# Sliding windows stored from the middle of a row: a 28-element shift between two channel halves

## The chip, the cores and the metric

The kernel runs on one core of a Trainium2 chip, alone. Its time is the device time of one execution in microseconds; a number for a kernel is the median over runs. All tensors are float32. Nothing is computed beyond copying, so TensorE has no work.

## The reference

An image batch is cut into overlapping windows of 8 x 8 pixels, 4 apart, and every window is written out with all of its channels:

```python
x: (16, 64, 64, 64)                     # batch, channels, height, width
n_h = n_w = (64 - 8) // 4 + 1           # 15
result = zeros((16, 15, 15, 64, 8, 8))
for i in range(15):
    for j in range(15):
        result[:, i, j] = x[:, :, 4*i:4*i+8, 4*j:4*j+8]
```

The input has 16.78 MB, the output 58.98 MB: 3600 windows (b, i, j) of 64 channels x 64 pixels, that is 16 KB each and contiguous in the output. Windows of one image follow each other by i and then j.

## The kernel before

**Where the input lies.** One tile `L` holds all of the input: 128 partitions = 2 channel halves (`ch`, 64 partitions each) x 16 images x 4 quarters of the height (`hq`); a partition has 32 channels x 16 rows x 64 columns, 128 KB. So a window row index i is 4*hq + s with a slot s of 0 to 3: for s = 0, 1, 2 the 8 pixel rows lie inside a quarter, for s = 3 the lower 4 of them lie in the next partition (next quarter), and quarter 3 has no such window.

**Loads.** The first 4 channels of each half (`FC`) come in by 8 DMAs of 64 partitions, ScalarE's queue for half 0 and SyncE's for half 1, into two of the four output buffers used as staging (`S`), partitions 32 to 95. The other 28 channels come in by loads of 8 partitions each straight into `L`, from SyncE's queue and from POOL's (`load`, L58); every row is 4 KB. The images are taken as two sets of 8 (`y`). The staging copies (L126) then move the 4 channels from `S` to `L`, half 0 on ScalarE and half 1 on VectorE, each in two instructions, one for each `y`.

**Stores.** Four buffers `G` of 128 partitions x 16 KB are filled in turn; each partition of a buffer is one whole window, 64 channels. A buffer is stored by one indirect DMA from POOL (`scatter`, L138), which sends each partition's 16 KB to the output row that an index tile names; rows out of bounds are dropped. There are up to eight DMAs of POOL in flight, each with its own semaphore.

**Filling.** Early tiles (`part`) need only one set of 8 images: 32-partition copies, 3 on ScalarE and 5 on VectorE (L196). Three of them come first for y = 0, three later for y = 1, alternating with plain tiles. In a tile of `unit`, a plain one (s = 0) holds slot 0 in its lower 64 partitions and slot 1 in the upper ones; a crossing one (s = 2) holds slots 2 and 3 at one column j. A half of the partitions has only half of the channels, so each 64-partition half of a tile is filled from both channel halves by `fill`: one copy stays in its partitions, the other goes across 64 partitions. ScalarE's copies are L158; VectorE's across are shuffles (L168), with a quarter of the channels going to ScalarE (L172). For slot 3 the lower 4 rows come by a shuffle that moves data one partition up (L161). The last column's slots 0 and 1 are stored by two plain SyncE DMAs of 64 partitions (32 to 95).

**Order.** Nothing but the program order, the buffers' turn and the scheduler of the framework sets the order: each engine works down its list, and a copy into a buffer waits until the store four tiles earlier has landed.

Of the kernel before, what the change touches and what calls it, by code (L numbers as in the profile page):

```python
# [10 lines left out]
def kernel(  # L11
# [19 lines left out]
    CH = 2  # L31
    HQ = P // (B * CH)
    CL = C // CH
    RB = H // HQ
    NSLOT = RB // ST
    NWIN = NH * NW
    CFREE = C * WS * WS
    HP = P // CH
    YB = 8
    NY = B // YB  # L40
    QP = YB * HQ
    assert HQ == 4 and WS == 2 * ST and QP == 32 and NSLOT == 4
# [22 lines left out]
    pi, tb, tq, tc_, th, idx, idx_y0, idx_y1, idx_lo, idx_hi = (  # L65
        itile(n) for n in ("pi", "tb", "tq", "tc", "th", "idx", "idx_y0", "idx_y1", "idx_lo", "idx_hi")
    )
    FAR = float(2 * B * NWIN)
# [8 lines left out]
    def tt(d, a, b, op):  # L77
        nc.vector.tensor_tensor(out=d[:, :], in0=a[:, :], in1=b[:, :], op=op)  # L78

    bits(tb, 2, B - 1)  # L80
    bits(tq, 0, HQ - 1)
    bits(tc_, 6, 1)
    mul(tb, tb, NWIN)
    mul(th, tq, NSLOT * NW)
    tt(tb, tb, th, ALU.add)
    mul(th, tc_, NW)
    tt(idx, tb, th, ALU.add)

    bits(th, 5, 1)
    mul(idx_y0, th, 1 - YB * NWIN)  # L90
    tt(idx_y0, idx_y0, idx, ALU.add)
    nc.vector.tensor_scalar(out=idx_y1[:, :], in0=idx_y0[:, :], scalar1=float(YB * NWIN), scalar2=None, op0=ALU.add)

    nc.vector.tensor_scalar(out=tq[:, :], in0=tq[:, :], scalar1=float(HQ - 1), scalar2=FAR, op0=ALU.is_equal, op1=ALU.mult)
    tt(th, tc_, tq, ALU.mult)
    tt(idx_hi, idx, th, ALU.add)
    nc.vector.tensor_scalar(out=tc_[:, :], in0=tc_[:, :], scalar1=-1.0, scalar2=1.0, op0=ALU.mult, op1=ALU.add)
    tt(th, tc_, tq, ALU.mult)
    tt(idx_lo, tb, th, ALU.add)
    mul(th, tc_, NW)  # L100
    tt(idx_lo, idx_lo, th, ALU.add)


    NG = 4
    G = [gpool.tile([P, C, WS, WS], f32, name=f"G{n}") for n in range(NG)]
    FC = C * WS * WS // (RB * W)
    S = [g.rearrange("p c r w -> p (c r w)").rearrange("p (c r w) -> p c r w", c=FC, r=RB) for g in G[NG - CH :]]
# [14 lines left out]
    for y in range(NY):  # L122
        for ch in range(CH):
            f = slice(QP + y * QP, QP + (y + 1) * QP)
            d = slice(ch * HP + y * QP, ch * HP + (y + 1) * QP)
            (nc.scalar.copy, nc.vector.tensor_copy)[ch](out=L[d, 0:FC, :, :], in_=S[ch][f])  # L126

    o_v = out.rearrange("b i j c r w -> (b i j) (c r w)")
    nxt = [min(p + 1, 31) for p in range(32)]

    o_q = out.rearrange("b i j c r w -> i j b (c r w)")
# [5 lines left out]
    def scatter(g, ix, j, s):  # L137
        st = nc.gpsimd.indirect_dma_start(  # L138
            out=o_v,
            out_offset=bass.IndirectOffsetOnAxis(ap=ix[:, 0:1], axis=0),  # L140
            in_=g.rearrange("p c r w -> p (c r w)"),
            in_offset=None,
            element_offset=(s * NW + j) * CFREE,
            bounds_check=B * NWIN - 1,
            oob_is_err=False,
        )
        free(st)

    def fill(g, half, s, j, lo, n, copies):

        d = slice(half * HP + lo, half * HP + lo + n)
        cols = slice(j * ST, j * ST + WS)
        for ch in (half, 1 - half):
            f = slice(ch * HP + lo, ch * HP + lo + n)
            cs = slice(ch * CL, (ch + 1) * CL)
            copy = copies[ch != half]
            if s < NSLOT - 1:
                copy(out=g[d, cs, :, :], in_=L[f, :, s * ST : s * ST + WS, cols])  # L158
            else:
                copy(out=g[d, cs, 0:ST, :], in_=L[f, :, s * ST : RB, cols])  # L160
                nc.vector.stream_shuffle(out=g[d, cs, ST:WS, :], in_=L[f, :, 0:ST, cols], mask=nxt)  # L161

    act, dve = nc.scalar.copy, nc.vector.tensor_copy
    same = list(range(32))


    def shf(out, in_):
        nc.vector.stream_shuffle(out=out, in_=in_, mask=same)  # L168

    def split(k, other):  # L170
        def both(out, in_):
            act(out=out[:, 0:k], in_=in_[:, 0:k])  # L172
            other(out=out[:, k:], in_=in_[:, k:])  # L173

        return both

    mix = split(CL // 4, shf)


    EARLY = 3  # L180
    ACT_C = 12
    at = 0

    def tile_():
        nonlocal at
        at += 1
        return G[(at - 1) % NG]

    def part(y, j):
        g = tile_()  # L190
        for d in range(P // QP):
            s, dj = d // NY, d % NY
            cols = slice((j + dj) * ST, (j + dj) * ST + WS)
            for ch in range(CH):
                f = (ch * NY + y) * QP
                (act if (2 * d + ch) % 3 == 0 else dve)(  # L196
                    out=g[d * QP : (d + 1) * QP, ch * CL : (ch + 1) * CL, :, :],
                    in_=L[f : f + QP, :, s * ST : s * ST + WS, cols],
                )
        scatter(g, (idx_y0, idx_y1)[y], j, 0)  # L200

    crossed = 0

    def unit(j, s, copies=(shf, mix)):
        nonlocal crossed
        g = tile_()
        if s == 0:
            fill(g, 0, 0, j, 0, HP, (act, copies[0]))
            fill(g, 1, 1, j, 0, HP, (act, copies[1]))
            scatter(g, idx, j, s)  # L210
        else:

            turn = 1 - crossed % 2
            crossed += 1
            fill(g, turn, s, j, 0, HP, (act, act))
            fill(g, 1 - turn, s + 1, j, 0, HP, (shf, mix))
            scatter(g, (idx_hi, idx_lo)[turn], j, s)

    for n in range(EARLY):
        part(0, 2 * n)  # L220
    plain = [(j, 0) for j in range(2 * EARLY, NW - 1)]
    cross = [(j, 2) for j in range(NW)]
    for n in range(EARLY):
        part(1, 2 * n)
        unit(*plain.pop(0), (dve, dve))
    while plain:
        for w in cross[:3]:
            unit(*w)
        cross = cross[3:]
        unit(*plain.pop(0), *([] if len(plain) else [(split(ACT_C, shf), split(ACT_C, dve))]))  # L230


    o_e = out.rearrange("b i j c r w -> j b i (c r w)")
    j = NW - 1
    for s in range(2):
        g = tile_()
        cols = slice(j * ST, j * ST + WS)
        for y in range(NY):
            d = slice(QP + y * QP, QP + (y + 1) * QP)
            for ch in range(CH):  # L240
                f = slice(ch * HP + y * QP, ch * HP + (y + 1) * QP)
                for c0, c1, copy in ((0, ACT_C, act), (ACT_C, CL, dve)):
                    copy(out=g[d, ch * CL + c0 : ch * CL + c1, :, :], in_=L[f, c0:c1, s * ST : s * ST + WS, cols])  # L243
        g_q = g.rearrange("p c r w -> p (c r w)")
        free(nc.sync.dma_start(out=o_e[j, :, s : s + (HQ - 1) * NSLOT + 1 : NSLOT], in_=g_q[QP : QP + HP]))


# [33 lines left out]
```

## Time and profile before

| | |
|---|---|
| median of 3 runs | 187.99 us (187.95 to 188.54) |
| profiled execution | 187.89 us |
| its span, first to last instruction | 186.1 us |
| VectorE, ScalarE, POOL busy | 146.8 us (79%), 146.5 us (79%), 47.7 us (26%) |
| DMA packets | 11300, 75.81 MB, mean 407 GB/s |
| POOL's queue, SyncE's, ScalarE's | 86.6%, 10.6%, 1.8% of 16 DMA engines' span |
| landing of a store after its issue on POOL | 9.3 to 15.0 us, median 11.7 |

An execution's time is its span and some 1.8 us around it. Busy shares are of the span; the share of a queue is the time that its packets took, of 16 engines. Line numbers (L158) are those of the kernel's file.

### The profile page before, as it was taken

To read this page: it belongs to the slowest core of one execution; us is meant where nothing else is said; L and a number is where in the kernel's file an instruction comes from. 1 tells how busy PE (TensorE), PEld (TensorE's weight loads), DVE (VectorE), ACT (ScalarE), POOL (GpSimd) and SP (SyncE) were. 2 spreads that over 40 slices of the span, in tenths; PEclk is the share of its full clock that TensorE was granted. 3 is DMA by queue.
4 is the path that set the end of the run, shared out by engine and by line. 5 is a ranking of instruction groups with operands and counts; after the bars stand their busy time and mean duration, and the time that the engine had idled before them with its cause. 6 is when DMAs were issued, how large, how long until landed. Compare 5 with 4: busy or idle time off the path is not lost.

```text
span 186.1 us, 575 instructions
## 1 busy us (share of the span) xinstructions
DVE 146.8 (79%) x205; ACT 146.5 (79%) x96; POOL 47.7 (26%) x50
## 2 busy tenths in 40 slices
DVE  5045008999998969799999999999999999998600
ACT  0069108997999989988899999998998899999600
POOL 7405222006335341422222222222222222223000
DMA  5999999999999999999999999999999999999994
GB/s 165 359 402 403 399 401 400 381 385 424 433 440 423 431 433 430 433 430 433 424 435 419 433 426 423 433 412 433 398 444 396 444 419 409 440 409 433 409 447 204
DMA packets 11300, 75.81 MB, mean 407 GB/s; under 512 B 3600, under 2 KB 3600, under 8 KB 7696
## 3 DMA queue, kind: packets, MB, share of 16 engines
q0 software_dynamic: 9296, 66.86, 86.6%
q1 hardware_dynamic: 1680, 7.86, 10.6%
q10 hardware_dynamic: 320, 1.05, 1.8%
q14 instruction: 4, 0.03, 0.0%
HBM read 16.78 MB, written 62.91 MB: 428 GB/s over the span
## 4 chain that ended last, share of the span: by engine, by line
DMA 41%; DVE 37%; issue 8%; ACT 5%; POOL 2%; ACTq 1%; POOLq 0%; DVEq 0%; PEldq 0%
DVE G L168 16%; DMA out_dram<-G,idx 14%; DMA out_dram<-G,idx_y 13%; DMA L<-in_x_dram 13%; DVE G L161 11%; DVE G L196 10%; ACT G L243 3%; POOL L L58 2%; ACT G L158 1%; ACT G L172 1%; ACTq L276 0%; DVE G L158 0%; POOLq L138 0%; POOL pi L69 0%; POOL out_dram L138 0%
## 5 line engine op out<-in xcount | busy, mean ns | idle before, releaser
L158 ACT COPY G<-L 64x2048 f32<-64x2048 f32 x46 | 87.2, 1896 | 5.8 <-DMA out_dram<-G,idx 3.7
L168 DVE STREAM_SHUFFLE G<-L 64x1024 f32<-64x1024 f32 (+4 forms) x39 | 53.0, 1358 | 1.2
L196 DVE COPY G<-L 32x2048 f32<-32x2048 f32 x30 | 36.6, 1220 | 14.9 <-DMA L<-in_x_dram 12.1
L196 ACT COPY G<-L 32x2048 f32<-32x2048 f32 x18 | 33.9, 1896 | 11.5 <-DMA L<-in_x_dram 10.4
L161 DVE STREAM_SHUFFLE G<-L 64x1024 f32<-64x1024 f32 x30 | 38.4, 1280 | 0.0
L138 POOL DMA_INDIRECT out_dram<-G,idx_y x6 | 10.7, 1776 | 26.7 <-DVE G L196 16.3
L58 POOL DMA_DIRECT2D L<-in_x_dram x16 | 11.9, 760 | 19.5 <-DMA L<-in_x_dram 19.0
L138 POOL DMA_INDIRECT out_dram<-G,idx_lo x8 | 7.7, 963 | 30.9 <-DVE G L161 12.0
L138 POOL DMA_INDIRECT out_dram<-G,idx x8 | 10.4, 1295 | 18.1 <-ACT G L158 9.3
L138 POOL DMA_INDIRECT out_dram<-G,idx_hi x7 | 6.7, 962 | 26.6 <-DVE G L161 19.0
L126 DVE COPY L<-G 32x4096 f32<-32x4096 f32 x2 | 4.6, 2284 | 8.2 <-DMA G<-in_x_dram 8.2
L172 ACT COPY G<-L 64x256 f32<-64x256 f32 (+2 forms) x21 | 10.2, 484 | 0.5
L126 ACT ACT_TABLE_LOAD x1 | 1.3, 1283 | 10.8 <-DMA G<-in_x_dram 10.8
L158 DVE COPY G<-L 64x2048 f32<-64x2048 f32 x6 | 7.3, 1222 | 0.2
L243 DVE COPY G<-L 32x1280 f32<-32x1280 f32 x8 | 6.5, 818 | 0.9 <-DMA out_dram<-G,idx_hi 0.8
L126 ACT COPY L<-G 32x4096 f32<-32x4096 f32 x2 | 7.2, 3604 | 0.0
L243 ACT COPY G<-L 32x768 f32<-32x768 f32 x8 | 6.6, 829 | 0.1
L168 DVE LOAD_MASK_SELECT G<-L x39 | 0.3, 8 | 1.4 <-DMA out_dram<-G,idx_y 1.0
L72 DVE TENSOR_SCALAR tb<-pi 128x1 int32<-128x1 int32 x1 | 0.2, 153 | 1.0 <-POOL pi L69 1.0
L173 DVE COPY G<-L 64x1280 f32<-64x1280 f32 x1 | 0.9, 874 | 0.0
L78 DVE TENSOR_TENSOR th<-tc,tq 128x1 int32<-128x1 int32 x2 | 0.3, 156 | 0.0
L75 DVE TENSOR_SCALAR th<-tc 128x1 int32<-128x1 int32 x2 | 0.3, 154 | 0.0
(21 smaller groups left out, 3.0 us busy)
## 6 DMA issues: line engine op xcount, KB each, us to landing
L<-in_x_dram POOLq DMA_DIRECT2D x10, 896.0 KB, 19.3
L<-in_x_dram SPq DMA_DIRECT2D x6, 768.0 KB
out_dram<-G SPq DMA_DIRECT2D x2, 1024.0 KB, 10.2
G<-in_x_dram ACTq DMA_DIRECT2D x4, 256.0 KB, 8.0
G<-in_x_dram SPq DMA_DIRECT2D x4, 256.0 KB, 8.7
L<-in_x_dram POOLq DMA_DIRECT2D x6, 128.0 KB, 18.2
out_dram<-G,idx POOLq DMA_INDIRECT x8, 13.2
out_dram<-G,idx_lo POOLq DMA_INDIRECT x8, 10.6
```

Of the source, the lines that this page charges most:

```text
L58: eng.dma_start(out=L[p0 : p0 + QP - HQ + 1 : HQ, c0:c1, :, :], in_=x_v[ch, y, q, :, c0:c1, :])
L75: nc.vector.tensor_scalar(out=d[:, :], in0=a[:, :], scalar1=float(m), scalar2=None, op0=ALU.mult)
L78: nc.vector.tensor_tensor(out=d[:, :], in0=a[:, :], in1=b[:, :], op=op)
L126: (nc.scalar.copy, nc.vector.tensor_copy)[ch](out=L[d, 0:FC, :, :], in_=S[ch][f])
L138: st = nc.gpsimd.indirect_dma_start(out=o_v, out_offset=bass.IndirectOffsetOnAxis(ap=ix[:, 0:1], axis=0), in_=g.rearrange("p c r w -> p (c ...
L158: copy(out=g[d, cs, :, :], in_=L[f, :, s * ST : s * ST + WS, cols])
L161: nc.vector.stream_shuffle(out=g[d, cs, ST:WS, :], in_=L[f, :, 0:ST, cols], mask=nxt)
L168: nc.vector.stream_shuffle(out=out, in_=in_, mask=same)
L172: act(out=out[:, 0:k], in_=in_[:, 0:k])
L173: other(out=out[:, k:], in_=in_[:, k:])
L196: (act if (2 * d + ch) % 3 == 0 else dve)(out=g[d * QP : (d + 1) * QP, ch * CL : (ch + 1) * CL, :, :], in_=L[f : f + QP, :, s * ST : s * S ...
L243: copy(out=g[d, ch * CL + c0 : ch * CL + c1, :, :], in_=L[f, c0:c1, s * ST : s * ST + WS, cols])
```

## The change

The two channel halves now lie 28 elements (7 window steps) apart within a partition's row: half 0 starts at element 28 of the tile `Lt`, half 1 at element 0. `LB` views all 128 partitions from element 0. Read through `LB` at column j + 7, the lower partitions give half 0 at column j and the upper ones half 1 at column j + 7: one copy over 128 partitions fills the first half of every partition's 16 KB. The lower partitions' second half is half 1 at column j; the upper partitions' second half is half 0 at column j + 8.

So a lower partition holds the whole window j, and an upper one the second channel half of window j + 7 and the first channel half of window j + 8, which follow each other in the output. The upper partitions therefore store 16 KB from the middle of an output row to the middle of the next. The index tiles count half rows (8 KB). The lower partitions take columns 0 to 6, the upper ones everything from the middle of column 7 to the middle of column 14; what is left over, the first half of column 7 and the second half of column 14, is stored by `singles` in rows of 8 KB. A tile has one slot s; slots 0, 1 and 2 go out in one scatter of 128 partitions, slot 3 in two of 64 partitions (`scatter_x`), since the rows of quarter 3 have to be dropped. Seven tiles are of slot 3. The store from SyncE's queue at the end is now slot 1 at column 6 and its partner.

```diff
-    L = lpool.tile([P, CL, RB, W], f32)
+    JL = NW // 2
+    SH = JL * ST
+    LF = CL * RB * W
+    Lt = lpool.tile([P, LF + SH], f32)
+    L = [Lt[ch * HP : (ch + 1) * HP, SH - ch * SH : SH - ch * SH + LF].rearrange("p (c r w) -> p c r w", c=CL, r=RB) for ch in range(CH)]
+    LB = Lt[:, 0:LF].rearrange("p (c r w) -> p c r w", c=CL, r=RB)
...
     def load(eng, ch, y, q, c0, c1):
-        p0 = ch * HP + y * QP + q
-        eng.dma_start(out=L[p0 : p0 + QP - HQ + 1 : HQ, c0:c1, :, :], in_=x_v[ch, y, q, :, c0:c1, :])
+        p0 = y * QP + q
+        eng.dma_start(out=L[ch][p0 : p0 + QP - HQ + 1 : HQ, c0:c1, :, :], in_=x_v[ch, y, q, :, c0:c1, :])
...
-            d = slice(ch * HP + y * QP, ch * HP + (y + 1) * QP)
-            (nc.scalar.copy, nc.vector.tensor_copy)[ch](out=L[d, 0:FC, :, :], in_=S[ch][f])
+            d = slice(y * QP, (y + 1) * QP)
+            (nc.scalar.copy, nc.vector.tensor_copy)[ch](out=L[ch][d, 0:FC, :, :], in_=S[ch][f])
...
+    def scatter_x(g, s, j):
+        for u in range(CH):
+            hp = slice(u * HP, (u + 1) * HP)
+            st = nc.gpsimd.indirect_dma_start(
+                out=out.rearrange("b i j c r w -> (b i j) (c r w)"),
+                out_offset=bass.IndirectOffsetOnAxis(ap=idx_r[0:HP, 0:1], axis=0),
+                in_=g[hp, :, :].rearrange("p h f -> p (h f)"),
+                in_offset=None,
+                element_offset=(s * NW + j + u * JL) * CFREE + u * HFREE,
+                bounds_check=B * NWIN - 1,
+                oob_is_err=False,
+            )
+            free(st)
...
+    def move(out, src, s, col, copy):
+        cols = slice(col * ST, col * ST + WS)
+        if s < NSLOT - 1:
+            copy(out=out, in_=src[:, :, s * ST : s * ST + WS, cols])
+        else:
+            copy(out=out[:, :, 0:ST, :], in_=src[:, :, s * ST : RB, cols])
+            nc.vector.stream_shuffle(out=out[:, :, ST:WS, :], in_=src[:, :, 0:ST, cols], mask=nxt)
...
+    def cell(s, j, copy=shf):
+        g = tile_()
+        move(win(g, 0, P, 0), LB, s, j + JL, act)
+        move(win(g, 0, HP, 1), L[1], s, j, act)
+        move(win(g, HP, HP, 1), L[0], s, j + JL + 1, act if s == NSLOT - 1 else copy)
+        if s < NSLOT - 1:
+            scatter(g, idx, s, j)
+        else:
+            scatter_x(g, s, j)
...
+    plain = [(s, j) for s in range(2) for j in range(EARLY, JL)] + [(2, j) for j in range(JL)]
+    plain.remove((1, JL - 1))
+    cross = [(NSLOT - 1, j) for j in range(JL)]
...
+    nc_, nt = len(cross), len(plain) + len(cross)
+    for n in range(nt):
+        cell(*(cross if (n + 1) * nc_ // nt > n * nc_ // nt else plain).pop(0))
...
+    singles(0)
+    singles(2)
+    last(1, JL - 1)
```

In the changed file the staging copies are L125, the early copies L196, plain copies and shuffles L172 and L167, crossing copies and shuffles L174 and L175, the scatters L137 and L150.

More of the change, by code (lines that the diff above doesn't have):

```diff
@@ L75, in mul @@
         nc.vector.tensor_scalar(out=d[:, :], in0=a[:, :], scalar1=float(m), scalar2=None, op0=ALU.mult)
[L77 to L100, printed above, removed]
@@ L104 @@
+    rows(idx, tb, 2, B - 1, CH * NWIN)
+    rows(idx, idx, 6, 1, NW)
+    bits(ta, 0, HQ - 1)
+    nc.vector.tensor_scalar(out=ta[:, :], in0=ta[:, :], scalar1=float(HQ - 1), scalar2=FAR, op0=ALU.is_equal, op1=ALU.mult)
+    add(idx_x, idx, ta)
+    rows(idx_r, tb, 2, B - 1, CH * NWIN)
+    mul(idx_r, idx_r, 1 / CH)
+    bits(ta, 0, HQ - 1)
+    nc.vector.tensor_scalar(out=ta[:, :], in0=ta[:, :], scalar1=float(HQ - 1), scalar2=FAR, op0=ALU.is_equal, op1=ALU.mult)
+    add(idx_r, idx_r, ta)
     NG = 4
-    G = [gpool.tile([P, C, WS, WS], f32, name=f"G{n}") for n in range(NG)]
@@ L106 @@
-    FC = C * WS * WS // (RB * W)
-    S = [g.rearrange("p c r w -> p (c r w)").rearrange("p (c r w) -> p c r w", c=FC, r=RB) for g in G[NG - CH :]]
+    G = [gpool.tile([P, CH, HFREE], f32, name=f"G{n}") for n in range(NG)]
+    FC = CFREE // (RB * W)
+    S = [g.rearrange("p h f -> p (h f)").rearrange("p (c r w) -> p c r w", c=FC, r=RB) for g in G[NG - CH :]]
     x_b = x.rearrange("b (ch cl) (hq r) w -> ch hq b cl (r w)", ch=CH, hq=HQ)
@@ L143, in scatter @@
             element_offset=(s * NW + j) * CFREE,
-            bounds_check=B * NWIN - 1,
-            oob_is_err=False,
+            **({} if n > 1 else dict(bounds_check=CH * B * NWIN - 1, oob_is_err=False)),
         )
         free(st)
[L149 to L161, printed above, removed]
+    def scatter_x(g, s, j):
[11 more added lines that the diff above has]
+            free(st)
@@ L163, with win @@
+    def win(g, p0, n, h):
+        return g[p0 : p0 + n, h, :].rearrange("p (c r w) -> p c r w", c=CL, r=WS)
     act, dve = nc.scalar.copy, nc.vector.tensor_copy
-    same = list(range(32))
     def shf(out, in_):
         nc.vector.stream_shuffle(out=out, in_=in_, mask=same)
[L170 to L180, printed above, removed]
@@ L191, in part @@
         for d in range(P // QP):
[L192 to L198, printed above, removed]
-                )
-        scatter(g, (idx_y0, idx_y1)[y], j, 0)
-    crossed = 0
@@ L204, in unit @@
[L204 to L245, printed above, removed]
+            s, u = d // CH, d % CH
@@ new lines, in part @@
+            for h in range(CH):
+                ch = h ^ u
+                col = j + (JL + h if u else 0)
+                src = L[ch][y * QP : (y + 1) * QP, :, s * ST : s * ST + WS, col * ST : col * ST + WS]
+                (act if (2 * d + h) % 3 == 0 else dve)(out=win(g, d * QP, QP, h), in_=src)
+        scatter(g, (idx_y0, idx_y1)[y], 0, j)
+    def cell(s, j, copy=shf):
[7 more added lines that the diff above has]
+            scatter_x(g, s, j)
@@ new lines, with singles @@
+    for n in range(EARLY):
+        part(0, n)
+    plain = [(s, j) for s in range(2) for j in range(EARLY, JL)] + [(2, j) for j in range(JL)]
+    plain.remove((1, JL - 1))
+    cross = [(NSLOT - 1, j) for j in range(JL)]
+    for n in range(EARLY):
+        part(1, n)
+        cell(*plain.pop(0), dve)
+    nc_, nt = len(cross), len(plain) + len(cross)
+    for n in range(nt):
+        cell(*(cross if (n + 1) * nc_ // nt > n * nc_ // nt else plain).pop(0))
+    def singles(s0):
+        g = tile_()
+        for h, s in enumerate((s0, s0 + 1)):
+            move(win(g, 0, P, h), LB, s, CH * JL, act)
+            scatter(g, idx_x if s == NSLOT - 1 else idx, s, JL, 1, h)
@@ new lines, in last @@
+    def last(s, j):
+        o_e = out.rearrange("b i j (h c) r w -> i b (j h c r w)", h=CH)
+        for u in range(CH):
+            g = tile_()
+            for y in range(NY):
+                for h in range(CH):
+                    ch = h ^ u
+                    col = j + (JL + h if u else 0)
+                    src = L[ch][y * QP : (y + 1) * QP, :, s * ST : s * ST + WS, col * ST : col * ST + WS]
+                    for c0, c1, copy in ((0, ACT_C, act), (ACT_C, CL, dve)):
+                        copy(out=win(g, QP + y * QP, QP, h)[:, c0:c1], in_=src[:, c0:c1])
+            at = (CH * j + u * NW) * HFREE
+            free(
+                nc.sync.dma_start(
+                    out=o_e[s : s + (HQ - 1) * NSLOT + 1 : NSLOT, :, at : at + CFREE].rearrange("i b f -> b i f"),
+                    in_=g[QP : QP + HP, :, :].rearrange("p h f -> p (h f)"),
+                )
+            )
```

33 lines of the change are left out of this document (21 added, 12 removed).

## The prediction

> **What bounds the kernel now.** I read the page's slices first, then the busy table by stage, the timeline of the first 60 us, the table of groups by form, and last the DMA queues of the final 2 us. The span is 186.1 us.
>
> The slices of the page; each is 4.65 us wide:
>
> ```profile
> DVE  5045008999998969799999999999999999998600
> ACT  0069108997999989988899999998998899999600
> ...
> DMA  5999999999999999999999999999999999999994
> GB/s 165 359 402 403 399 401 400 381 385 424 433 440 423 431 433 430 433 430 433 424 435 419 433 426 423 433 412 433 398 444 396 444 419 409 440 409 433 409 447 204
> ```
>
> The DMA row is 9 in every slice but the first and the last. VectorE and ScalarE are full too, but only from slice 17 on, and the transfer rate hardly moves when they fill up: the transfers set the time, and the engines only have to keep them fed. The table by stage puts rates to it (last two columns: share of the 16 DMA engines, GB/s):
>
> ```profile
> 24.00:28.00 4.00, 0.00 (x0) 0.00 (x0) 1.27 (x2) 1.00 1.03 400
> 40.00:44.00 4.00, 3.91 (x4) 4.00 (x3) 1.40 (x1) 1.00 1.06 387
> 80.00:90.00 10.00, 9.66 (x18) 8.70 (x8) 1.92 (x2) 1.00 1.01 431
> 100.00:140.00 40.00, 39.36 (x63) 38.55 (x28) 8.66 (x9) 1.00 1.00 422
> 182.40:184.20 1.80, 0.00 (x0) 0.00 (x0) 0.00 (x0) 1.00 0.84 355
> ```
>
> Loads (4 KB rows) run at 400 GB/s, stores (16 KB rows) at 431. Nothing is idle between them: 16.78 MB of loads end near 45.4 us (16.2 MB by 44 us in the 4 us windows, the rest at 390), and the first store is issued before that. So any microsecond in which no transfer is queued, and any loss of rate, goes to the end in full. How tight the handover is shows in the timeline:
>
> ```profile
> 10.83 1.28 ACT L126 ACT_TABLE_LOAD   x1 [10.83 <-DMA G<-in_x_dram]
> 11.82 4.60 DVE L126 COPY L<-G 32x4096 f32<-32x4096 f32 x2 [8.17 <-DMA G<-in_x_dram]
> 12.13 7.23 ACT L126 COPY L<-G 32x4096 f32<-32x4096 f32 x2
> ...
> 28.47 16.98 ACT L196 COPY G<-L 32x2048 f32<-32x2048 f32 x9 [9.11 <-DMA L<-in_x_dram]
> 28.49 24.92 DVE L196 COPY G<-L 32x2048 f32<-32x2048 f32 x20 [12.07 <-DMA L<-in_x_dram]
> ...
> 42.14 1.40 POOL L138 DMA_INDIRECT out_dram<-G,idx_y  x1 [9.72 <-ACT G L196]
> ```
>
> The staging copies (L126) run at 11 to 19 us, while both engines have nothing else. At 28.47 the lower images' first channel half has landed and the window copies begin: 9 on ScalarE at 1.887 each, 20 on VectorE at 1.246 each (gaps included). Store 1 needs seven of ScalarE's nine: 28.47 + 13.2 = 41.7, and it is issued at 42.14, from where about 2.6 us pass until its bytes move.
>
> The prices by form:
>
> ```profile
> L158 ACT COPY G<-L 64x2048 f32<-64x2048 f32 x46 | 87.2, 1896 | 5.8 <-DMA out_dram<-G,idx 3.7 <-DVE G L161 0.6 <-DMA out_dram<-G,idx_hi 0.4
> L161 DVE STREAM_SHUFFLE G<-L 64x1024 f32<-64x1024 f32 x30 | 38.4, 1280 | 0.0
> L196 ACT COPY G<-L 32x2048 f32<-32x2048 f32 x18 | 33.9, 1896 | 11.5 <-DMA L<-in_x_dram 10.4 <-DMA out_dram<-G,idx_y 0.8
> L172 ACT COPY G<-L 64x768 f32<-64x768 f32 x2 | 1.7, 829 | 0.1
> ```
>
> A copy on 32 partitions costs what one on 64 does (1896 ns): the time goes by elements per partition, so I price 128 partitions the same.
>
> **Part 1, the copies: cheaper, and hidden.** A plain tile now takes ScalarE two copies (128 and 64 partitions, 2 x 1.90 = 3.8 us) and VectorE one shuffle (2.43 us), against 4.87 us for its 2.10 MB at 431 GB/s. A crossing tile takes ScalarE 3 x 1.04 (1024 elements, interpolated between 829 and 1896 ns) and VectorE 3 x 1.28 = 3.84 us; before, VectorE had about 4.85 us of shuffles for each crossing tile, whose 112 rows (1.84 MB) move in 4.26 us, so from 80 us on it fell slowly behind. What that relief can be worth is the difference between 431 and 422 GB/s from 100 to 180 us, 80 x 9/431 = 1.7 us at the most, and nothing if the rate falls for another reason. I take 1.0. The bytes are the same, 58.98 MB out. The index arithmetic (25 small instructions for 20, about 0.15 us each) and POOL's seven extra scatters (0.96 us each, engine 26% busy) lie under transfers: nothing.
>
> **Part 2, the staging copies move.** In the instruction order that the changed program is built with, they are no longer first. ScalarE's first one now waits for all loads of its half and images (queues of POOL and SP), not for its staging loads alone, and so does VectorE's; the two halves being flat slices of one tile, the dependency tracking sees an overlap that the bytes don't have. So the table load and the staging copy go onto the path at 28.47: 1.28 + 7.23/2 = 4.9 us. Both engines' window copies queue behind it, since VectorE's first copy waits for that ScalarE copy. From 33.4 us: ScalarE's seventh window copy ends at 33.4 + 7 x 1.887 = 46.6, store 1 is issued at 47.0, its bytes move at 49.6. The loads are over at 45.4: **a first hole of 4.2 us**, where there was none.
>
> A second follows. Stores 1 to 3 (6.29 MB) last 14.6 us, to 64.2. Store 3's buffer is also staging room: two of its VectorE copies wait until ScalarE's second staging copy has read it, which now stands after all nine window copies: 33.4 + 17.0 + 3.6 = 54.0. Then VectorE has these two (56.5), one copy for tile 4, its own second staging copy (2.3), and four more copies: 56.5 + 1.25 + 2.3 + 5.0 = 65.0. Store 4 is issued at 65.1, moves at 67.7: **3.5 us of hole**. From there tiles come every 3.8 to 5.7 us with stores 5 and 6 already queued behind; no further hole. Sum 7.7 us, all on the path.
>
> **Part 3, crossing stores come in two.** Each of seven crossing tiles is stored by two scatters of 64 partitions, 0 to 63 and then 64 to 127, 48 valid rows (0.79 MB) each. Before, every store of this size spanned both halves; no row shows a store from one half only. At the full 431 GB/s one takes 1.82 us and the price is nothing. The other bound: if a half is served by half of the SBUF's paths, 216 GB/s, 3.65 us, 1.82 more, 14 times: 25.5 us. What rows are near? The final SP stores have 64 partitions, but 32 to 95:
>
> ```profile
> q1 hardware_dynamic: 48, 0.66, 81.3%
> ```
>
> From 182.4 to 184.3 this queue alone holds 81% of the 16 engines, so 64 rows are spread over all of them, four each; two half stores would then stand one behind the other on every engine, not side by side on two sets. The nearest one-sided rows are the loads of the upper half: POOL saw three of them land at 19.08, 24.93 and 31.12 us, 0.92 MB every 5.9 to 6.2 us, some 150 GB/s, well below the half rate, with the other half's loads beside them making up the 400. I take that a one-sided store runs at less than full rate, and three quarters of the extra, since an engine that is ahead already reads the second half while another is on the first: 14 x 1.4 = 19.6 us.
>
> [...]
>
> **Smaller terms.** Loads of the lower half now land 112 bytes into the row. No row shows such loads; I take 0 and keep up to 1.5 us for the range. [...] A store that starts in mid-row might go as two 8 KB packets: by the two rates (164 ns for 4 KB, 608 for 16 KB on one engine), 8 KB is 312, 2.6% on 41.9 MB, 2.5 us; I take 0. The four 8 KB scatters at the end cost 0.24 us by that.
>
> **Sum** on the profiled execution: 186.1 + 7.7 - 1.0 + 19.6 = 212.4 us of span; 1.8 us lie around the span (187.89 for 186.1, and the median of the runs is 187.99): 214.2, say **214 us**.
>
> **Rivals.**
> A, the forecast (chance 0.70): both holes, and one-sided stores below full rate; its own range is 203 to 222, from half of the 25.5 to all of it with the smaller terms.
> B, halves side by side (0.24): the second scatter's rows overlap the first's and nothing is lost; the holes stay: 186.1 + 7.7 - 1.0 + 1.8 = 194.6 us, to 198 with the smaller terms. For it: the loads of two halves do run side by side. Against: one queue in order, and the 81%.
> C, not slower (0.04): the staging copies run at 12 us after all, because those waits are met early; it is decided by whether ScalarE's first L125 copy starts before 28 us. Then store 1 leaves at 42.1, no hole opens, and, halves side by side, VectorE's relief of 1.7 us is left: 186.1 - 1.7 + 1.8 = 186.2 us. Against it: the loads that it waits for are those whose landing at 28.47 started the window copies before.
> The remaining 0.02 is for worse than A, such as engines 0 to 7 alone carrying the lower half.
>
> The range takes in B and A with their bounds: 193 to 222. A measurement of this kernel can tell about 0.3% from no change: faster 0.03, within 0.01, slower 0.96.
>
> **What would show it.** ScalarE's table load and first L125 copy at 28 us and not at 11; first scatter at 47; DMA slices of 5 or less near 46 to 49 us and again near 65; then dips of the GB/s row to near 220 each time the pair L150 reaches the queue, with landing times up, VectorE no longer full. If the late slices stay at 420 to 431, B holds. If no slice near 47 is empty, part 2 is wrong. If crossing dips are absent and the end still is beyond 200 us, the rate of all mid-row stores has fallen, and part 3's reason is wrong.

## The result, and the profile after

| | before | after |
|---|---|---|
| median of 4 runs each | 188.12 us | 238.84 us (238.29 to 239.69) |
| ratio, 95% interval | | 1.270 (1.265 to 1.275) |
| span of the profiled execution | 186.1 us | 237.9 us |

The change costs 50.7 us. The prediction's sign and both of its mechanisms came, but its 214 us and its upper end of 222 us were too low. The page's slices of the kernel after, each 5.95 us wide:

```profile
DVE  5000019987999844854145443336446423046200
ACT  0000099999699998686334663625835626266200
...
DMA  6999999749869999999999998978799888889620
GB/s 203 365 407 400 398 398 380 272 196 421 354 262 399 441 441 419 419 419 304 333 412 295 309 325 298 314 248 289 231 325 325 245 286 287 310 286 342 275 94 18
```

Three things differ from before. The DMA row has two holes (7 and 4, then 8 and 6, between 42 and 72 us), the two that were predicted. From 107 us on the rate is mostly near 300 instead of 420, although the DMA row still shows 7 to 9. And the end runs out slowly (6, 2, 0), where before had one short slice. VectorE and ScalarE are half empty from about 95 us on. The table by stage (busy us of VectorE, ScalarE and POOL with counts, then PEclk, DMA share, GB/s):

```profile
44.00:48.00 4.00, 3.93 (x5) 3.96 (x4) 0.00 (x0) 1.00 0.45 165
48.00:52.00 4.00, 3.94 (x4) 3.98 (x3) 3.13 (x2) 1.00 0.30 131
60.00:64.00 4.00, 3.90 (x4) 2.75 (x2) 1.32 (x1) 1.00 0.78 330
64.00:68.00 4.00, 3.91 (x4) 3.95 (x3) 1.03 (x1) 1.00 0.61 262
68.00:72.00 4.00, 3.94 (x4) 3.98 (x3) 2.99 (x2) 1.00 0.77 328
...
120.00:140.00 20.00, 8.06 (x9) 9.80 (x7) 3.70 (x4) 1.00 0.98 326
140.00:160.00 20.00, 8.76 (x10) 8.82 (x6) 3.73 (x4) 1.00 0.88 294
...
220.00:230.00 10.00, 1.64 (x2) 1.66 (x2) 0.00 (x0) 1.00 0.50 211
230.00:238.00 8.00, 0.00 (x0) 0.00 (x0) 0.00 (x0) 1.00 0.06 25
```

Read the last two columns against each other. In the first five lines the rate is low because the share is low: nothing was queued. The empty share of these windows is 4 x (0.55 + 0.70 + 0.22 + 0.39 + 0.23) = 8.4 us. From 120 to 140 the share is 0.98 and the rate 326: the engines are busy, and their packets take longer: of the 398 rows of 16 KB that begin there, 77 took over 1 us, where before none did. From 140 on both are low. In the last 8 us the share is 0.06, on the mean one engine's worth of 16: a few engines still work while the others have finished.

The queues' shares give the same split for the whole span. Before they sum to 99.0% of 186.1, that is 184.2 us of packets per engine and 1.9 us empty. After:

```profile
q0 software_dynamic: 9696, 66.86, 76.6%
q1 hardware_dynamic: 1680, 7.86, 8.3%
q10 hardware_dynamic: 320, 1.05, 1.4%
...
out_dram<-G,idx POOLq DMA_INDIRECT x17, 22.8
out_dram<-G,idx_r POOLq DMA_INDIRECT x14, 21.8
```

86.3% of 237.9 is 205.3 us of packets and 32.6 us empty: for the same bytes the packets take 21.1 us longer, and the engines are empty for 30.7 us more. The last two lines (median us from issue to landing) show that not only the crossing stores (`idx_r`) land late but the plain ones too, 22.8 us where before had 13.2. The timeline of the kernel after answers part 2:

```profile
29.63 1.28 ACT L125 ACT_TABLE_LOAD   x1 [29.63 <-DMA Lt<-in_x_dram]
30.92 3.60 ACT L125 COPY Lt<-G 32x4096 f32<-32x4096 f32 x1
34.56 16.96 ACT L196 COPY G<-Lt 32x2048 f32<-32x2048 f32 x9
...
48.21 2.25 POOL L137 DMA_INDIRECT out_dram<-G,idx_y  x1 [16.71 <-ACT G L196]
...
51.54 3.60 ACT L125 COPY Lt<-G 32x4096 f32<-32x4096 f32 x1
...
66.97 1.86 POOL L137 DMA_INDIRECT out_dram<-G,idx_y  x1 [5.65 <-ACT G L172]
```

The table load and the staging copy stand behind all loads of their images, at 29.63 (28.47 predicted); store 1 is issued at 48.21 (47.0), store 4 at 66.97 (65.1).

### The profile page after: what moved, and what is told of

Same layout as the page of the kernel before. It is cut to its first block, busy times and chain, and to the rows that moved or that the text cites. A ratio compares the mean times of both kernels' runs of the same rounds, so it can differ in the third digit from the quotient of the medians.

```text
span 237.9 us, 478 instructions
## 1 busy us (share of the span) xinstructions
DVE 110.1 (46%) x134; ACT 130.4 (55%) x82; POOL 54.0 (23%) x59
## 3 DMA queue, kind: packets, MB, share of 16 engines
q10 hardware_dynamic: 320, 1.05, 1.4%
## 4 chain that ended last, share of the span: by engine, by line
DMA 68%; DVE 12%; ACT 10%; issue 2%; ACTq 1%; SPq 0%; POOL 0%; DVEq 0%; POOLq 0%
DMA out_dram<-G,idx_r 27%; DMA out_dram<-G,idx 25%; DMA Lt<-in_x_dram 9%; DVE G L196 8%; ACT G L196 6%; DMA out_dram<-G,idx_y 5%; ACT Lt L125 3%; DMA G<-in_x_dram 3%; DVE G L175 2%; DVE G L172 2%; DVE Lt L125 1%; ACTq L280 1%; ACT L125 1%; SPq L111 0%; POOL out_dram L150 0%
## 5 line engine op out<-in xcount | busy, mean ns | idle before, releaser
L172 ACT COPY G<-Lt 128x2048 f32<-128x2048 f32 (+1 forms) x31 | 58.5, 1897 | 29.3 <-DMA out_dram<-G,idx_r 14.6
L196 DVE COPY G<-Lt 32x2048 f32<-32x2048 f32 x30 | 36.5, 1218 | 32.4 <-ACT Lt L125 31.8
L174 ACT COPY G<-Lt 64x1024 f32<-64x1024 f32 (+1 forms) x22 | 23.0, 1044 | 25.6 <-DMA out_dram<-G,idx 24.5
L196 ACT COPY G<-Lt 32x2048 f32<-32x2048 f32 x18 | 33.9, 1896 | 2.5 <-DVE Lt L125 2.2
L137 POOL DMA_INDIRECT out_dram<-G,idx x17 | 18.5, 1089 | 63.6 <-ACT G L172 36.2
L175 DVE STREAM_SHUFFLE G<-Lt 64x1024 f32<-64x1024 f32 (+1 forms) x22 | 28.1, 1279 | 0.6
L167 DVE STREAM_SHUFFLE G<-Lt 64x2048 f32<-64x2048 f32 x11 | 26.9, 2447 | 0.1
L150 POOL DMA_INDIRECT out_dram<-G,idx_r x14 | 12.7, 904 | 37.9 <-ACT G L174 34.7
L137 POOL DMA_INDIRECT out_dram<-G,idx_y x6 | 11.7, 1943 | 35.4 <-ACT G L196 16.7
L125 ACT ACT_TABLE_LOAD x1 | 1.3, 1283 | 29.6 <-DMA Lt<-in_x_dram 29.6
L167 DVE LOAD_MASK_SELECT G<-Lt x11 | 0.2, 14 | 36.5 <-DMA out_dram<-G,idx_r 21.4
L175 DVE LOAD_MASK_SELECT G<-Lt x22 | 0.3, 14 | 34.5 <-DMA out_dram<-G,idx 22.5
L63 POOL DMA_DIRECT2D Lt<-in_x_dram x16 | 9.9, 630 | 20.7 <-DMA Lt<-in_x_dram 19.9
L125 ACT COPY Lt<-G 32x4096 f32<-32x4096 f32 x2 | 7.2, 3604 | 0.0
L125 DVE COPY Lt<-G 32x4096 f32<-32x4096 f32 x2 | 4.6, 2284 | 0.1
L172 DVE COPY G<-Lt 64x2048 f32<-64x2048 f32 x3 | 3.7, 1221 | 0.1
L137 POOL DMA_INDIRECT out_dram<-G,idx_x x1 | 1.0, 977 | 0.3 <-issue 0.3
## 6 DMA issues: line engine op xcount, KB each, us to landing
out_dram<-G,idx POOLq DMA_INDIRECT x17, 22.8
```

The costliest lines, as they stand in the source:

```text
L63: eng.dma_start(out=L[ch][p0 : p0 + QP - HQ + 1 : HQ, c0:c1, :, :], in_=x_v[ch, y, q, :, c0:c1, :])
L125: (nc.scalar.copy, nc.vector.tensor_copy)[ch](out=L[ch][d, 0:FC, :, :], in_=S[ch][f])
L137: st = nc.gpsimd.indirect_dma_start(out=o_h, out_offset=bass.IndirectOffsetOnAxis(ap=ix[:, 0:1], axis=0), in_=g[:, h : h + n, :].rearrange ...
L150: st = nc.gpsimd.indirect_dma_start(out=out.rearrange("b i j c r w -> (b i j) (c r w)"), out_offset=bass.IndirectOffsetOnAxis(ap=idx_r[0:H ...
L172: copy(out=out, in_=src[:, :, s * ST : s * ST + WS, cols])
L174: copy(out=out[:, :, 0:ST, :], in_=src[:, :, s * ST : RB, cols])
```

## The experiments

The medians, in us; each ratio is against the kernel before in the same session (187.7 to 188.1), with its 95% interval:

| run | median | ratio |
|---|---|---|
| e1_stage_first | 229.44 | 1.220 (1.215 to 1.225) |
| e3_two_full | 201.28 | 1.069 (1.065 to 1.073) |
| e5_both | 193.12 | 1.028 (1.023 to 1.032) |
| e4_before_split | 235.0 (lowest) | none |
| e6_last_lower | 193.25 | 1.029 (1.026 to 1.031) |
| e7_no_copies | 228.73 | 1.220 (1.215 to 1.226) |
| e8_no_copies_full | 192.22 | 1.023 (1.021 to 1.025) |
| e9_whole_rows | 193.16 | 1.028 (1.025 to 1.030) |
| e10_singles_early | 192.92 | 1.028 (1.025 to 1.032) |
| e11_cross_last | 209.04 | 1.114 (1.109 to 1.118) |
| e12_cross_last_full | 193.25 | 1.029 (1.026 to 1.032) |
| e13_one_scatter | 191.08 | 1.015 (1.009 to 1.020) |

### The two suspects, each alone and together

e1_stage_first takes part 2 away: loads and staging copies are declared independent, so the staging copies run early again.

```diff
-        eng.dma_start(out=L[ch][p0 : p0 + QP - HQ + 1 : HQ, c0:c1, :, :], in_=x_v[ch, y, q, :, c0:c1, :])
+        ld = eng.dma_start(out=L[ch][p0 : p0 + QP - HQ + 1 : HQ, c0:c1, :, :], in_=x_v[ch, y, q, :, c0:c1, :])
+        fills.append(ld)
...
-            (nc.scalar.copy, nc.vector.tensor_copy)[ch](out=L[ch][d, 0:FC, :, :], in_=S[ch][f])
+            fills.append((nc.scalar.copy, nc.vector.tensor_copy)[ch](out=L[ch][d, 0:FC, :, :], in_=S[ch][f]))
+    for ld in fills:
+        tc.declare_no_dep(ld.ins, group="fills", reason="loads and staging copies write channels of their own")
+        tc.add_to_no_dep_group("fills", ld.ins)
```

> The changed kernel, with the loads into the big tile and the staging copies told that they touch different bytes, so that the staging copies run at 11 to 19 us again. Theory T (two holes in the transfers, one at 45 and one at 64 us, 8.6 us of empty engines by the DMA shares of the stages; the rest of the loss from the one-sided stores): the first scatter is back near 43 us, no slice near 46 to 66 us is below 400 GB/s, and the time falls by 7 to 9 us, to 230 to 232. Rival S (the holes cost nothing, since the later stores, limited by something else, would have waited anyway): 236 to 239.

e3_two_full takes part 3 away: the two scatters of a crossing tile name all 128 partitions, and each drops the other half's rows by an index out of bounds.

```diff
+    bits(ta, 6, 1)
+    mul(ta, ta, FAR)
+    add(idx_r0, idx_r, ta)
+    bits(ta, 6, 1)
+    nc.vector.tensor_scalar(out=ta[:, :], in0=ta[:, :], scalar1=-FAR, scalar2=FAR, op0=ALU.mult, op1=ALU.add)
+    add(idx_r1, idx_r, ta)
...
-            hp = slice(u * HP, (u + 1) * HP)
+            ix = (idx_r0, idx_r1)[u]
...
-                out_offset=bass.IndirectOffsetOnAxis(ap=idx_r[0:HP, 0:1], axis=0),
-                in_=g[hp, :, :].rearrange("p h f -> p (h f)"),
+                out_offset=bass.IndirectOffsetOnAxis(ap=ix[:, 0:1], axis=0),
+                in_=g[:, :, :].rearrange("p h f -> p (h f)"),
```

> The changed kernel, with each crossing tile still stored by two scatters, but each of them over all 128 partitions, the first dropping the rows of the upper half and the second those of the lower. The staging copies stay late. Theory T (a 64-partition scatter spreads rows of one half over all 16 engines, two engines then meet on one path to SBUF, rows take up to twice as long and the engines fall out of step; with 128 partitions named, every engine keeps to its own partitions): no packets at twice the time, rate 415 to 431 to the end, 194 to 198 us. Rival R1 (rows that start in the middle of an output row are slow wherever they come from): 225 or more. Rival R2 (dropped rows leave the engines unequal work): even more rows are dropped in each scatter, so 238 or more.

e5_both makes both edits.

> Both edits: staging copies early, crossing tiles in two scatters of 128 partitions. Theory T: neither holes nor one-sided stores are left, and VectorE is relieved: 185.5 to 188.5 us, the kernel before within 1.3%. If a third cause is in the change (half-row starts, loads 112 bytes into the row), 190 or more.

The four kernels make a square, and its sides agree. The late staging costs 238.8 - 229.4 = 9.4 us with one-sided stores and 201.3 - 193.1 = 8.2 without. The one-sided stores cost 238.8 - 201.3 = 37.5 us with the late staging and 229.4 - 193.1 = 36.3 without. Both parts are confirmed as mechanisms; part 2 has the size that was given (7.7), part 3 is nearly twice its 19.6 and beyond its bound of 25.5. With both taken away 5 us remain that the prediction doesn't have; for the same reason e3 (201.3) and e5 (193.1) lie above what was expected of them, 194 to 198 and 185.5 to 188.5. In the table by stage of e1_stage_first the early holes are gone and the late loss is there as in the kernel after:

```profile
44.00:48.00 4.00, 3.73 (x5) 2.18 (x2) 2.11 (x2) 1.00 1.08 439
48.00:52.00 4.00, 3.91 (x4) 3.95 (x3) 1.34 (x1) 1.00 1.02 432
...
64.00:68.00 4.00, 1.71 (x3) 3.79 (x3) 2.48 (x2) 1.00 1.03 442
...
160.00:180.00 20.00, 8.73 (x10) 10.56 (x7) 4.68 (x5) 1.00 0.88 286
```

and in that of e5_both it is gone too:

```profile
120.00:140.00 20.00, 13.35 (x17) 15.07 (x12) 5.85 (x6) 1.00 1.01 417
140.00:160.00 20.00, 12.62 (x16) 14.74 (x12) 5.42 (x6) 1.00 1.01 416
160.00:180.00 20.00, 7.85 (x10) 13.03 (x12) 5.30 (x6) 1.00 1.01 413
```

The queues' shares of e1_stage_first, and then of e5_both:

```profile
q0 software_dynamic: 9696, 66.86, 79.6%
q1 hardware_dynamic: 1680, 7.86, 8.8%
q10 hardware_dynamic: 320, 1.05, 1.3%
...
q0 software_dynamic: 10592, 66.86, 85.0%
q1 hardware_dynamic: 1680, 7.86, 10.4%
q10 hardware_dynamic: 320, 1.05, 1.8%
```

By these shares, e1 has 203.1 us of packets and 23.3 us empty, e5 185.6 and 5.3. So the 35.5 us between their spans are 17.5 us of longer packets and 18.0 us in which engines had nothing to do.

### Is it the side, and not the mid-row start or the dropped rows?

e4_before_split puts one-sided stores into the kernel before, whose rows are whole and not dropped: each of its eight plain stores goes as partitions 0 to 63 and then 64 to 127.

```diff
-            scatter(g, idx, j, s)
+            for u in range(CH):
+                scatter(g, idx, j, s, slice(u * HP, (u + 1) * HP), u)
```

> The kernel before, with its eight plain tiles stored by two scatters of 64 partitions each (0 to 63, 64 to 127); no row of these is dropped and all start at the beginning of an output row. Theory T: 16 one-sided stores of 1.05 MB, 2.43 us at the full rate; rows at twice the time would add 2.43 each, 39 us, three quarters of it 29, and engines out of step some 10 to 25 more: 215 to 250 us. Rivals R1 and R2: nothing that they blame is in this kernel, 188 to 190.

Its four runs scatter from 235.0 to 243.5 us, so only the lowest is used, and no ratio is given. 235.0 - 188.1 = 46.9 us for 16 stores of 1.05 MB, at least 2.9 us each, where doubling their 2.43 us would cost 2.4. One-sidedness alone makes the loss, larger than a halved rate, and neither a start in mid-row nor a dropped row is needed for it.

e6_last_lower asks whether it is a matter of POOL's scatters: in the kernel before, the two final SyncE stores take partitions 0 to 63 instead of 32 to 95.

```diff
-            d = slice(QP + y * QP, QP + (y + 1) * QP)
+            d = slice(y * QP, (y + 1) * QP)
...
-        free(nc.sync.dma_start(out=o_e[j, :, s : s + (HQ - 1) * NSLOT + 1 : NSLOT], in_=g_q[QP : QP + HP]))
+        free(nc.sync.dma_start(out=o_e[j, :, s : s + (HQ - 1) * NSLOT + 1 : NSLOT], in_=g_q[0:HP]))
```

> The kernel before; only its last two stores, 64 partitions each from SyncE's queue, use partitions 0 to 63 of their buffers instead of 32 to 95. Theory T says that the side of SBUF matters, whoever issues: 2 x 1.05 MB at half rate would take 2.4 us more each, of which the stores still queued from POOL may cover a part: 190 to 193 us, with packets of this queue near 1.2 us and a longer drain after the last ScalarE copy. Rival U (it is POOL's indirect scatter of 64 rows that is slow, not the side): 188 us, as before.

Two stores of 1.05 MB cost 193.25 - 187.78 = 5.5 us, 2.7 each. Near the end the table by stage of the kernel before has

```profile
180.00:184.00 4.00, 0.00 (x0) 0.00 (x0) 0.00 (x0) 1.00 1.00 422
```

and that of e6_last_lower:

```profile
180.00:184.00 4.00, 0.00 (x0) 0.00 (x0) 0.00 (x0) 1.00 0.94 262
184.00:186.00 2.00, 0.00 (x0) 0.00 (x0) 0.00 (x0) 1.00 1.13 246
186.00:190.00 4.00, 0.00 (x0) 0.00 (x0) 0.00 (x0) 1.00 0.40 164
```

Up to 186 us the share is full and the rate 246 to 262: the engines are busy and their packets take longer. So the side counts for SyncE's stores as for POOL's. The prediction's half rate is 216 GB/s; the 246 measured here, with some of POOL's rows among them, is 14% above it.

The trace has the time of each packet, and a packet here is one 16 KB row. Of the 128 rows of the two stores in e6, 64 took 0.61 to 0.78 us and 64 took 1.06 to 1.36; in the kernel before, none took more than 0.64. All rows that begin between 184 and 186.6 us take 1.2 us. The last 32 begin after eight of the last store's 16 engines have reported, and they take 0.61 again. So a one-sided row was slow while all engines were at work on that half, and ran at full speed when only eight were left. The rows beside them pay as well: 30 rows of POOL's last stores, which span both halves, took 1.08 to 1.38 us, where in the kernel before no row of POOL's took a full microsecond.

### Why more than twice the time?

My first explanation was that the late landings hold the buffers, so that engines starve for tiles. e7_no_copies is e1 without the copies that fill the buffers after the first three plain cells (those tiles are stored with old content); then none of these stores waits for a copy. e8_no_copies_full is the same for e5.

```diff
-        move(win(g, 0, P, 0), LB, s, j + JL, act)
-        move(win(g, 0, HP, 1), L[1], s, j, act)
-        move(win(g, HP, HP, 1), L[0], s, j + JL + 1, act if s == NSLOT - 1 else copy)
+        if copy is dve:
+            move(win(g, 0, P, 0), LB, s, j + JL, act)
+            move(win(g, 0, HP, 1), L[1], s, j, act)
+            move(win(g, HP, HP, 1), L[0], s, j + JL + 1, copy)
```

> The changed kernel with early staging copies (229.4 us), and without the copies that fill the plain and crossing tiles from the fourth plain tile on: the stores are the same in number, size, side and order, but wait for nothing except POOL's eight semaphores, since their buffers are not written again. Theory T, second half (a store lands with its slowest engine; with four buffers the faster engines then run dry, and this, not the doubled rows alone, is some 15 us of the loss): shares of DMA time near 1 to the end of the stores and 205 to 218 us. Rival V (buffers do not matter, the path to SBUF is the limit through and through): 226 to 231.

> As the one without copies, with the crossing tiles stored by two scatters of 128 partitions (193.1 us with its copies). All theories: the transfers are the limit there and the copies are hidden, 190 to 194 us. If it falls to 188 or less, copies cost something in the fixed kernel.

The explanation fell: 228.7 against 229.4, and 192.2 against 193.1. Taking the buffers' waits away saves less than 1 us in either. What remains in e7's table by stage is nearly the transfers alone:

```profile
120.00:140.00 20.00, 0.00 (x0) 0.00 (x0) 3.68 (x4) 1.00 1.00 332
140.00:160.00 20.00, 0.00 (x0) 0.00 (x0) 3.72 (x4) 1.00 1.01 337
...
180.00:200.00 20.00, 1.30 (x2) 6.54 (x4) 2.96 (x3) 1.00 0.62 228
...
220.00:225.00 5.00, 0.00 (x0) 0.00 (x0) 0.00 (x0) 1.00 0.07 28
```

To 160 us the engines are all busy at 332 to 337 GB/s, and then part of them stands empty. The waits of e7 (us in total, times, longest) name what holds POOL there:

```profile
POOL out_dram L155 <- DMA out_dram<-G,idx: 33.5, 6, 7.0
...
POOL out_dram L142 <- DMA out_dram<-G,idx_r: 15.2, 4, 4.2
```

Where the copies are gone it is the landing of older stores, since POOL never has more than eight in flight (eight is also the most in the kernels before and after). And a store lands with the last of its 16 reports, which the trace has as single events and which I read as one from each engine: in the kernel after, one store's reports come from 126.41 to 140.23 us, and the ScalarE copy that waits for this store begins at 140.25. In the plain stores before the first crossing one these reports lie within some 2 us of each other. In e1 POOL's stores that land after 130 us have 14 to 20 us from the first report to the last, and in the kernel after those that land after 145 us have 14.6 to 20.2. So an engine that is ahead runs out of work while a late one still has several stores to do. With the buffers' limit gone in e7, the engines drift up to 31 us apart, but the late ones need as long as before: the span is 225.7 us, and 226.4 in e1.

e11_cross_last leaves the stores one-sided and changes only the order: the seven crossing tiles come after all plain tiles and the 8 KB stores. e12_cross_last_full is its control, with 128-partition scatters.

```diff
-    for n in range(nt):
-        cell(*(cross if (n + 1) * nc_ // nt > n * nc_ // nt else plain).pop(0))
+    for w in plain:
+        cell(*w)
+    singles(0)
+    singles(2)
+    for w in cross:
+        cell(*w)
```

> The changed kernel with early staging copies (229.4 us), with its seven crossing tiles, still in one-sided scatters of 64 partitions, moved behind all plain tiles and the 8 KB stores. Theory T in its exact form (a one-sided row takes twice the time, nothing else): the order is of no importance, 14 x 1.82 = 25.5 us above the kernel with both edits, 218 to 220, here as in the old order; the old order, at 229.4, contradicts this already. Theory W (the plain rows between one-sided stores pay as well, once engines are out of step and meet on a path that only one of them should use): without plain rows in between 213 to 221. Theory X (each one-sided store has a price of its own of some 2.6 us, wherever it stands): 227 to 231.

> The control for the one with the crossing tiles last: the same order, crossing tiles in two scatters of 128 partitions. All theories: 191 to 195, as the order alone does little while the transfers are never idle.

The same 14 one-sided stores now cost 209.0 - 193.25 = 15.8 us instead of 36.3: 1.1 us each, less than the 1.82 of a halved rate. The order alone is worth 20 us, and a fixed price per store, whether 2.6 or 1.82, is out. e11's table by stage: plain stores run at full rate as long as no one-sided store is ahead of them, and the loss begins with the first.

```profile
120.00:140.00 20.00, 6.76 (x8) 14.68 (x9) 6.02 (x7) 1.00 1.01 431
140.00:160.00 20.00, 16.08 (x25) 13.02 (x13) 7.21 (x8) 1.00 1.03 362
160.00:180.00 20.00, 11.65 (x19) 9.73 (x10) 5.46 (x6) 1.00 0.87 266
```

Here the reports of a crossing store, from the second on, come in two groups of eight: of one, eight between 161.7 and 163.0 us and eight between 170.5 and 172.7. So half of the engines get ahead of the other half. If these then read one half of the partitions while the others read the other, that would be the partial overlap; no run shows it directly. In e1, where plain stores follow, the reports spread without a clear split into eight and eight.

By the queues' shares, the 15.8 us from e12 to e11 split as those from e5 to e1 did: 7.7 us of longer packets and 8.0 us empty (96.9% of 191.8 us in e12, 93.3% of 207.5 in e11). Two parts of nearly the same size are what eight engines with the whole loss and eight with none would give; the trace does not name the engines, so this is not shown. That rows of stores from both halves are slowed beside one-sided ones is shown: by e6 above, and in e11 by SyncE's two stores from 32 to 95, which run beside the last crossing ones and of whose 128 rows 21 took 1.0 to 1.27 us (none in e12). What decides which engine loses, why the order matters as much as it does, and whether two engines meet on one path, as theories T and W have it, these runs do not settle.

### The 5 us that remain

e9_whole_rows is e5 with the upper partitions' stores moved half a row on, so that every 16 KB store starts at the beginning of a row; the halves that it writes there are swapped.

```diff
-    rows(idx, idx, 6, 1, NW)
+    rows(idx, idx, 6, 1, NW + 1)
...
-                element_offset=(s * NW + j + u * JL) * CFREE + u * HFREE,
+                element_offset=(s * NW + j + u * JL + u) * CFREE,
```

> The kernel with both edits (193.1 us), with the upper partitions' 16 KB stored half a row further on, so that every store of 16 KB starts at the beginning of an output row (channel halves then come out swapped there, the bytes being as many). What is left against the kernel before is 5 us. Rival R1 in its weak form (rows that start in the middle cost a few per cent on half the engines): 188 to 190. Otherwise (the 5 us come from dropped rows and from the order at the end): 192 to 194.

e10_singles_early is e5 with the four 8 KB stores right after the early tiles and the plain tiles last.

```diff
+    singles(0)
+    singles(2)
     for n in range(nt):
-        cell(*(cross if (n + 1) * nc_ // nt > n * nc_ // nt else plain).pop(0))
+        cell(*(cross if (nt - n) * nc_ // nt > (nt - n - 1) * nc_ // nt else plain).pop(0))
...
-    singles(0)
-    singles(2)
```

> The kernel with both edits (193.1 us), with the 8 KB stores right after the early tiles and the crossing tiles spread so that plain tiles come last: the last stores are then plain ones from POOL and the two from SyncE. If the order at the end is what is left of the 5 us (POOL's 8 KB rows draining last, then 1.9 us in which SyncE waits at the closing barrier): 189 to 191. If the rest is in the dropped rows and in the rate from 100 us on: 192 to 193.5.

Both equal e5 (193.2 and 192.9 for 193.1): neither the mid-row start nor the order of the end costs anything that can be seen.

e13_one_scatter is e9 with one scatter of 128 partitions for each crossing tile, which the row offset allows; 32 rows are dropped.

```diff
-        for u in range(CH):
-            ix = (idx_r0, idx_r1)[u]
+        for ix in (idx_r0,):
...
-                element_offset=(s * NW + j + u * JL + u) * CFREE,
+                element_offset=(s * NW + j) * CFREE,
```

> The kernel with both edits and whole-row stores (193.2 us; channel halves of the upper partitions come out swapped), with each crossing tile stored by one scatter of 128 partitions, in which only the 32 rows of quarter 3 are dropped, instead of two that drop 80 each. If the two scatters and their dropped rows are what is left of the 5 us: 189 to 190.5. If not (the closing wait of 1.9 us, and engines that end apart for another reason): 192 to 193.5.

193.2 to 191.1, between the two ranges expected: the second scatter, with the rows that it drops, costs 2.1 us in all, 0.3 for each of seven. A part of the rest is at the close, in SyncE's waits (us in total, times, longest), of e5_both

```profile
SPq L292 <- PEq L292: 2.4, 2, 1.9
```

and of the kernel before:

```profile
SPq L276 <- PEq L276: 0.7, 2, 0.5
```

That is 1.7 us more, and it stands behind the last store: from the last landing to the end of the span e5 takes 3.1 us and the kernel before 0.9. Why is open. e13 still is 3.1 us above the kernel before and takes 2.8 us at the close, 1.8 more than before; some 1.3 us is unexplained. No version here beats the kernel before.

## Why the prediction was right or wrong

The 50.7 us are, by the square: 5.0 (e5 against before), 8.2 (late staging, in e3), 37.5 (one-sided stores).

**Part 2, right.** The two holes show at the predicted places and sum to 8.4 us in the windows, 8.2 to 9.4 by the runs, 7.7 predicted. Each step came: the table load at 29.6, store 1 at 48.2, ScalarE's second staging copy behind nine window copies at 51.5, store 4 at 67.0. All times are 1 to 2 us later than given; 1.2 of it is that ScalarE's loads landed at 29.63, later than the 28.47 read from before.

**Part 3, the step that failed.** The mechanism was right: 64 partitions from one side are slow, and rival B (halves side by side, 194.6) fell with e4 and e6. Its size was not: 14 x 1.4 = 19.6 us stands against 36.3 to 37.5, 2.6 us a store in place of 1.4, and outside the stated bound of 14 x 1.82 = 25.5. The bound took a one-sided store at half rate as the worst, and its three quarters took an overlap of the two halves. For stores that stand together this is about what happens: 15.8 us in e11. In the kernel's order two things come on top that the sum left out. Rows of full stores pay too, where they run beside one-sided ones (e6). And the 16 engines don't share the loss evenly: the packets lengthened by 17.5 us on the mean of the engines (e5 to e1), but the slowest engines set the end, and the others stood empty for another 18.0 us. That the 17.5 is near the 19.6 is partly luck, since rows of full stores are in it. "Nothing is idle between them", read from before, was carried over to a kernel in which it no longer held. The upper bound should have had a term for plain stores beside one-sided ones; as it was, the range stopped at 222. The 203 at the lower end of A does not follow from its own terms: half of the 25.5 gives 207.

That half of the paths serves a half of the partitions, behind the bound's 216 GB/s, was an assumption: e6 shows a rate of 246 to 262 with some of POOL's rows among them, and no run shows paths. e11's 15.8 us are 62% of the doubling's 25.5, and the interleaved order's 36.3 are more than all of it.

**Part 1, no gain.** The relief of VectorE came (46% busy after, 58% in e5, 79% before), the 1.0 us did not. In e5 VectorE is busy for 13 of the 20 us from 120 to 140, and the rate is 417; in the kernel before it was full at 420 to 423:

```profile
120.00:140.00 20.00, 19.70 (x31) 18.95 (x15) 4.22 (x5) 1.00 1.00 420
140.00:160.00 20.00, 19.72 (x31) 18.15 (x13) 3.85 (x4) 1.00 1.01 423
```

In e12 it is busy for 6.2 us of the same 20, at 423. So VectorE was not what held the late rate below 431. In e11, which stores no crossing tile before 140 us, the rate is 431 to 432 from 60 to 140; in e12, with the same order, it is 423 from 100 to 140, so what lowers it is not shown. That the copies are hidden was right: e8 saves 0.9 us by leaving most of them out.

**The smaller terms, right but for one.** Loads that land 112 bytes on: 400 and 398 GB/s in slices 4 to 6 (399 to 403 before), and their last packet ends at 46.9 us, at 46.0 before; from 4 to 44 us the rate is 390 to 395 in e10 to e12, whose loads land the same way, and 393 before. So nothing clear of noise; the 1.5 us that the range kept for them was my own allowance, and no run shows it. Mid-row stores: 0 (e9). POOL's extra scatters were put at nothing as lying under transfers; in the kernel after their price can't be told apart from part 3, but as 128-partition scatters seven of them cost 2.1 us. The 1.7 us in the closing wait was not foreseen.

**Rivals and signs.** C (staging early after all) was decided by ScalarE's first L125 copy, which began at 30.9 and not before 28. Of the marks, the holes, the dips and the longer landings came; "dips to near 220 each time" did not: the rate falls once and stays mostly near 300.

## What to carry to other kernels

Store from all 128 partitions, also where half of the rows aren't wanted: a second scatter of this kind, with its dropped rows, cost 2.1 us for seven tiles here; naming 64 partitions instead cost 36 more. Where one-sided stores can't be avoided, put them together at the end (15.8 us) and not between full ones (36.3). When transfers set the end, price a slow transfer by the slowest DMA engine and not by the mean, and look at the last slices of the DMA row: a share of 0.06 is one engine's worth of 16.

## What the runs showed of the hardware

- While two SyncE stores of 64 partitions from 0 went out, with POOL's last rows among them and the engines busy, the rate was 246 to 262 GB/s; with the same stores in partitions 32 to 95 it was 422 from 180 to 184 us, and 355 when they were alone (e6 and before).
- Half of the rows of these stores took about twice the 0.61 us of a row in the kernel before, and the last 32, with eight engines left, took 0.61 again; rows of full stores beside them took up to 1.38 us (e6).
- Between and after one-sided stores the 16 engines reported one store up to 20 us apart (e1) and up to 31 us (e7), and the rate of the whole mix was 332 to 337 GB/s with the DMA share full (e7).
- In a run of one-sided stores the engines' reports split into two groups of eight, 3 to 16 us apart (e11).
- Nothing was lost by 16 KB stores that start in mid-row (193.1 us, and 193.2 in e9), nor by 4 KB load rows that land 112 bytes on (398 to 400 GB/s).
